# Feed forwards and output projection with the tokens stationary and 1024 weight columns moving

## The chip, the cores and the metric

One core of a Trainium2 chip runs the kernel. The metric is the device time of one execution in microseconds; lower is better. Times before are the median of three runs, beside one execution taken with the hardware profiler.

## What is computed

One layer on 256 tokens of width 2048, all in float32. Feed forwards have a hidden width of 5632.

```python
def swiglu(h, w_gate, w_up, w_down):
    return (jax.nn.silu(h @ w_gate) * (h @ w_up)) @ w_down

x = x + 0.5 * swiglu(rmsnorm(x, ffn1_norm), ffn1_w_gate, ffn1_w_up, ffn1_w_down)
h = rmsnorm(x, mix_norm)
rq, rk, rv, rg, aq, ak, av, iq, ik, iw = split(h @ w_in)
...   # retention on rq, rk, rv gated by rg; attention on the best 64 keys by an index score
x = x + concatenate([ro, ao]) @ w_out
x = x + 0.5 * swiglu(rmsnorm(x, ffn2_norm), ffn2_w_gate, ffn2_w_up, ffn2_w_down)
return rmsnorm(x, final_norm)
```

## The kernel before

Weights stream from DRAM once, in loads of 1 MB (`load`, SyncE's queue, three buffers `raw`). They are used in pieces of up to 1024 columns of 128 rows. Products keep float32 precision by splitting each number in a rounded part and a rest: `split(i)` lets ScalarE write the rounded part `hi` of piece i (L214) and VectorE the rest `lo` (L215), each with five buffers. A product is then hi x hi + hi x lo + lo x hi.

`mm_cols` (L137 with its partner L139, or L136 where a sum ends) does almost all products: a block of 128 weight columns is stationary, and the activations move, transposed, as 512 columns: 256 tokens of the rounded part and 256 of the rest. A 512 column product with the weights' `hi` and a 256 column product with their `lo` make one pair for each k tile and block. The result has the hidden or model columns in the partitions and the tokens along the row; the two halves of its bank are added when it is read. `mm_rows` (L154 to L156) does three small projections of the mix the other way around: 128 tokens are stationary, and 272 or 512 weight columns move.

x lies transposed in eight tiles of two k tiles. A feed forward takes its hidden columns in two halves, each of 11 chunks of 256: gate and up as two accumulators (`evac`: ScalarE copies one half of the bank to `b`, L315, VectorE adds the other, L317), scaling by the norm's row `r_of` (`row_of` builds it with TensorE), Silu, product, and the split of the result (`hs`). After the 11 chunks come eight chunks of 256 model columns (`down`), added to x; in the second half `split_x` and `square_x` make the next norm's inputs, and `add_squares` sums squares over the partitions with TensorE. The mix follows with its projections and small products, then the output projection, the second feed forward and `finish`, which scales x and sends it out in eight transfers.

The order on each engine is the program's: `split` runs four pieces ahead (two at the very start), then `run_step(i)` issues the functions that are due at step i (the work registered with `after`, stages of a function by `yield`), then piece i's products. So a function at step i stands on ScalarE and VectorE behind the split of piece i + 4, and on TensorE between the products of pieces i - 1 and i. PSUM is in two pools, two accumulators of two banks and four single banks, handed out anew for each use.

```python
        while n_split < min(n, i + ahead + 1):
            split(n_split)
            n_split += 1
        run_step(i)
        pieces[i]["mm"](*split_of.pop(i))
```

Of the kernel before, what the change touches and what calls it, by code (L numbers as in the profile page):

```python
# [19 lines left out]
P = 128  # L20
T = 256          # tokens
D = 2048         # model width
KT = D // P      # 16
FF = 5632
NCH = FF // 256  # 22 chunks of 256 hidden columns
HCH = NCH // 2   # 11 chunks in each half
HKT = 2 * HCH    # 22 k tiles in each half
# [18 lines left out]
def layer(ctx: ExitStack, tc: tile.TileContext, a: dict, out: bass.AP):  # L46
# [7 lines left out]
    p_acc = ctx.enter_context(tc.tile_pool(name="p_acc", bufs=2, space=PSUM))  # L54
    p_sm = ctx.enter_context(tc.tile_pool(name="p_sm", bufs=4, space=PSUM))
# [16 lines left out]
    gains = new(one, [P, 4 * KT + NH], F32, "gains")  # L72
    cst = new(one, [P, 4 + NH], F32, "cst")
    x = [new(one, [P, 2, T], F32, f"x{c}") for c in range(KT // 2)]
    xg = {}

# [1 line left out]
    loads = []   # lists of (offset, source)  # L78
# [7 lines left out]
    # a function may be a generator of stages; it yields the steps from one stage to the next  # L86
# [14 lines left out]
    class Chunk:  # L101
        """Where the products of a chunk of columns add up: a bank for each block of 128."""
        acc = None

        def get(self):
            if self.acc is None:
                self.acc = new(p_acc, [P, 2, 512], F32, "acc")
            return self.acc
# [4 lines left out]
    class LastChunk:  # L113
        """The same, with the first block complete before the last piece's products for the second"""

        banks = None

        def bank(self, b):
            if self.banks is None:
                self.banks = two_banks()  # L120
            return self.banks[b]

    def mm_cols(chunk, blocks, kts, rhs, first, last):
        """W[k, 128 cols] stationary; the split activations [k, hi | lo] move."""

        def go(hi, lo):
            order = [(i, b) for i in range(len(kts)) for b in range(blocks)]
            if last and isinstance(chunk, LastChunk):
                order.sort(key=lambda ib: ib[1])
            for i, b in order:  # L130
# [12 lines left out]
    def mm_rows(chunk, n, kts, rhs, first, last):  # L143
        """Tokens stationary; W[k, n cols] moves."""
# [14 lines left out]

    def block(src, l0, l1, width):  # L160
        """k tiles l0 to l1 of a chunk, which lie in DRAM as one block"""
        return src[P * l0 * width:P * l1 * width].rearrange("(p n) -> p n", p=P)

    def stream(src, kts, width, per_load, per_piece, rhs, chunk, maker, arg):
        """One chunk of columns over all its k tiles."""
# [8 lines left out]
        return len(pieces)   # the step after the chunk's last  # L174

    def stream_pair(srcs, rhs, chunks):
        """The first two chunks side by side, while x is loaded."""
        for k0 in range(0, KT, 4):
            w = 2 if k0 == 0 else 4
            parts = []  # L180
            for k in range(k0, k0 + 4, w):
                pre = list(range(k // 2, (k + w) // 2))
                parts += [lambda c=c: load_x(c) for c in pre]
                for m in range(2):
                    off = m * 1024 + (k - k0) * 256
                    at = (k % 8) * 256
                    parts.append((off, block(srcs[m], k // 8 * 8, k // 8 * 8 + 8, 256)[:, at:at + w * 256]))
                    pieces.append(dict(load=len(loads), off=off, n=w * 256, x=pre if m == 0 else [],
                                       mm=mm_cols(chunks[m], 2, list(range(k, k + w)), rhs, k == 0, k + w == KT)))
            loads.append(parts)  # L190
        return len(pieces) - 1, len(pieces)
# [12 lines left out]
    def split(i):  # L204
# [4 lines left out]
        for c in p.get("x", []):  # L209
            split_x(c, 0)  # L210
# [8 lines left out]
    s2 = {}  # L219

    def split_x(c, norm):
        """x * gain of two k tiles, split, for the next projections."""
        t = new(one, [P, 2, 512], F32R, f"xg{c}")
        for j in range(2):
            g = gains[:, norm * KT + 2 * c + j:norm * KT + 2 * c + j + 1]
            S.activation(t[:, j, :T], x[c][:, j], AF.Copy, scale=g)  # L226
            V.scalar_tensor_tensor(t[:, j, T:], x[c][:, j], g, t[:, j, :T].bitcast(F32), op0=OP.mult, op1=OP.subtract)  # L227
        xg[c] = t

    def square_x(c, norm):  # L230
# [671 lines left out]
```

## Time and profile before

| | |
|---|---|
| median of 3 runs | 1932.77 us (1932.54 to 1933.04) |
| the profiled execution's span, first to last instruction | 1931.7 us |
| TensorE busy (matmul records) | 1914.8 us, 99% |
| VectorE, ScalarE busy | 1207.8 us (63%), 924.9 us (48%) |
| read from DRAM | 352.63 MB, 184 GB/s over the span |

The profiled execution's own time is known by its span alone; the median of the runs is 1.07 us longer. Engines are named PE (TensorE matmul), PEld (its weight loads, which overlap the matmuls), DVE (VectorE), ACT (ScalarE), SP (SyncE). A line of a group reads: line of the kernel, engine, operation, written tile <- read tiles, shapes, count, then the busy time in us and the mean of one in ns, then the engine's idle time before them and what ended it. A line of the timeline reads: start in us, length in us, engine, line, operation, count of merged instructions, and in brackets the idle time before it and its releaser. Matmul records overlap, and their ends are modelled.

### The profile page before, as it was taken

The numbers are of one execution on the slowest core, as the hardware profiler recorded it, in microseconds if no ns is written. First come the engines' busy times: TensorE is split into PE (matmuls) and PEld (weight loads), VectorE is DVE, ScalarE is ACT, GpSimd is POOL, SyncE is SP. The second block draws the span as 40 slices with busy tenths as digits, with TensorE's granted clock in tenths as the row PEclk, the third lists the DMA queues.
The fourth block names the chain that finished last, engine by engine and source line by source line (L and its number), as shares of the span: only waits on it lengthen the run. The fifth ranks groups of instructions, "written<-read, shape, count | busy, mean of one in ns | idle before, by whom it ended". The sixth has DMA issues, their size and how long they took to land.

```text
span 1931.7 us, 26692 instructions
## 1 busy us (share of the span) xinstructions
PE 1914.8 (99%) x10936; PEld 1672.2 (87%) x10936; DVE 1207.8 (63%) x1444; ACT 924.9 (48%) x1127; POOL 5.3 (0%) x14
## 2 busy tenths in 40 slices
PE   8999999999999999999999999999999999999997
PEld 7888888888888888988888888888888888888886
DVE  7675655555656666688755766565655556655554
ACT  7444443344444445656544555444443344444442
POOL 0000000000000000000000000000000000000000
PEclk9999999999999999999999999999999999999999
DMA  7555555555555555545544555555555555555552
GB/s 287 187 184 196 178 178 189 197 192 182 194 182 184 180 188 202 177 156 196 175 153 158 187 179 191 182 194 182 189 180 182 194 188 193 187 184 191 179 181 104
DMA packets 53050, 356.44 MB, mean 185 GB/s; under 512 B 6048, under 2 KB 6048, under 8 KB 14144
## 3 DMA queue, kind: packets, MB, share of 16 engines
q1 hardware_dynamic: 52416, 353.52, 53.5%
q8 instruction: 85, 1.39, 0.3%
q0 software_dynamic: 368, 1.19, 0.2%
q14 instruction: 37, 0.30, 0.0%
q10 hardware_dynamic: 144, 0.04, 0.0%
HBM read 352.63 MB, written 2.10 MB: 184 GB/s over the span
## 4 chain that ended last, share of the span: by engine, by line
PE 99%; DVE 0%; DMA 0%; ACT 0%; issue 0%; DVEq 0%
PE acc L137 62%; PE acc L139 30%; PE acc L136 2%; PE acc L155 1%; PE acc L156 1%; PE acc L154 1%; PE sm L137 1%; PE sm L583 0%; PE sm L631 0%; PE sm L139 0%; DVE x L390 0%; DMA gains<-in_gains 0%; PE sm L724 0%; PE sm L700 0%; PE sm L662 0%; PE sm L267 0%
## 5 line engine op out<-in xcount | busy, mean ns | idle before, releaser
L137 PE MATMUL acc<-xg,hi 128*128 128x512 f32 x3504 | 1230.2, 395 | 5.8 <-DVE xg L227 5.8
L215 DVE TENSOR_TENSOR lo<-raw,hi 128x1024 fp32r<-128x1024 f32 (+2 forms) x686 | 817.2, 1194 | 665.9 <-ACT hi L214 664.2
L214 ACT ACTIVATE hi<-raw 128x1024 fp32r<-128x1024 f32 (+2 forms) x686 | 705.8, 1033 | 795.3 <-PE acc L137 754.2
L139 PE MATMUL acc<-xg,lo 128*128 128x256 f32 x3285 | 929.7, 283 | 0.0
L137 PEld LDWEIGHTS acc<-xg,hi 128*128 128x128 f32 x3504 | 652.6, 188 | 149.3 <-ACT hi L214 5.8
L139 PEld LDWEIGHTS acc<-xg,lo 128*128 128x128 f32 x3285 | 618.9, 188 | 5.0 <-DVE lo L215 0.4
L137 PE MATMUL acc<-mid,hi 128*128 128x512 f32 x1620 | 569.0, 398 | 0.0
L139 PE MATMUL acc<-mid,lo 128*128 128x256 f32 x1542 | 433.0, 281 | 0.0
L137 PEld LDWEIGHTS acc<-mid,hi 128*128 128x128 f32 x1620 | 302.0, 188 | 71.0 <-DVE mid L757 0.2
L139 PEld LDWEIGHTS acc<-mid,lo 128*128 128x128 f32 x1542 | 291.3, 189 | 1.6
L325 ACT ACTIVATE s<-e 128x512 f32<-128x512 f32 x44 | 27.8, 632 | 82.1 <-DVE e L323 82.1
L136 PE MATMUL acc<-xg,lo 128*128 128x256 f32 x219 | 61.1, 279 | 0.0
L317 DVE TENSOR_TENSOR e<-acc,b 128x512 f32<-128x512 f32 x88 | 60.1, 683 | 0.0
L315 ACT ACTIVATE b<-acc 128x512 f32<-128x512 f32 x88 | 51.1, 581 | 3.2 <-PE acc L137 3.2
L136 PEld LDWEIGHTS acc<-xg,lo 128*128 128x128 f32 x219 | 41.2, 188 | 5.0
L226 ACT ACTIVATE xg<-x,gains 128x256 fp32r<-128x256 f32 x48 | 21.5, 500 | 41.8 <-DVE x L808 19.5
L490 ACT ACTIVATE b<-e 64x512 f32<-64x512 f32 (+2 forms) x46 | 28.1, 612 | 15.6 <-DVE e L480 15.0
L154 PE MATMUL acc<-hi,xg 128*128 128x512 f32 (+1 forms) x96 | 34.9, 364 | 0.0
L155 PE MATMUL acc<-lo,xg 128*128 128x512 f32 (+1 forms) x96 | 34.5, 359 | 0.0
L156 PE MATMUL acc<-hi,xg 128*128 128x512 f32 (+1 forms) x96 | 34.5, 359 | 0.0
L331 DVE TENSOR_TENSOR e<-e,s 128x512 f32<-128x512 f32 x44 | 30.4, 692 | 1.5
L335 DVE TENSOR_TENSOR mid<-e,mid 128x512 fp32r<-128x512 f32 x44 | 30.1, 685 | 0.0
(149 smaller groups left out, 661.0 us busy)
## 6 DMA issues: line engine op xcount, KB each, us to landing
raw<-in_wgu SPq DMA_DIRECT2D x172, 1024.0 KB, 4.8
raw<-in_wd SPq DMA_DIRECT2D x64, 1024.0 KB, 4.8
raw<-in_wd SPq DMA_DIRECT2D x32, 768.0 KB, 4.2
raw<-in_w_out SPq DMA_DIRECT2D x16, 1024.0 KB, 4.8
raw<-in_w_iq SPq DMA_DIRECT2D x8, 1024.0 KB, 4.8
raw<-in_w_aq SPq DMA_DIRECT2D x8, 1024.0 KB, 4.8
raw<-in_w_rk SPq DMA_DIRECT2D x8, 1024.0 KB, 4.9
raw<-in_w_rq SPq DMA_DIRECT2D x8, 1024.0 KB, 4.9
```

Source lines behind the costliest of these rows:

```text
L136: TE.matmul(acc[:, T:], lhsT=lo[:, c:c + P], rhs=r[:, :T], start=False, stop=False)
L137: TE.matmul(acc, lhsT=hi[:, c:c + P], rhs=r, start=st, stop=sp)
L139: TE.matmul(acc[:, T:], lhsT=lo[:, c:c + P], rhs=r[:, :T], start=False, stop=False)
L154: TE.matmul(o, lhsT=h, rhs=hi[:, i * n:(i + 1) * n], start=st, stop=False)
L155: TE.matmul(o, lhsT=h, rhs=lo[:, i * n:(i + 1) * n], start=False, stop=False)
L156: TE.matmul(o, lhsT=l, rhs=hi[:, i * n:(i + 1) * n], start=False, stop=sp)
L214: S.activation(hi[:, :p["n"]], raw, AF.Copy)
L215: V.tensor_tensor(lo[:, :p["n"]], raw, hi[:, :p["n"]].bitcast(F32), op=OP.subtract)
L315: S.activation(b, acc[:, :, T:], AF.Copy)
L317: V.tensor_tensor(g, acc[:, :, :T], b, op=OP.add)
L331: V.tensor_tensor(u, u, sil[c], op=OP.mult)
L335: V.tensor_tensor(h[:, :, T:], u, h[:, :, :T].bitcast(F32), op=OP.subtract)
```

## The change

The feed forwards and the output projection go over to `mm_wide`: 128 tokens are stationary, 1024 weight columns move as two products of 512 into the two banks of a token tile. A piece is one k tile of 1024 columns. A chunk is 512 gate and 512 up columns; a feed forward has two parts of 6 and 5 chunks, and `down` and the output projection have two halves of 1024 model columns. PSUM is two fixed sets of four banks, used in turn; in the mix one set serves as the two accumulators (`pair`) and the other as the four single banks (`small`).

Results now lie by token. `hidden` multiplies them with the norm's factor per token, so no row is needed there, and TensorE transposes the gated product back, a step later, into the chunk's own set, for the split. x lies by token too: x is loaded a second time in that layout, `grow` adds to it, squares are summed by ScalarE along the row, and `turn_x` transposes it into the banks just read, for `split_x`. For norm 0 the transposed x is loaded into passing buffers. The output has another layout, and the last gain is loaded broadcast over the partitions.

```diff
-    p_acc = ctx.enter_context(tc.tile_pool(name="p_acc", bufs=2, space=PSUM))
-    p_sm = ctx.enter_context(tc.tile_pool(name="p_sm", bufs=4, space=PSUM))
+    psum = ctx.enter_context(tc.tile_pool(name="psum", bufs=1, space=PSUM))
...
+    sets = [[new(psum, [P, 2, 512], F32, f"set{s}{t}") for t in range(2)] for s in range(2)]
...
+    def mm_wide(acc, _, kts, rhs, first, last):
+        def go(hi, lo):
+            for i, kt in enumerate(kts):
+                r = rhs(kt)
+                st, sp = first and i == 0, last and i == len(kts) - 1
+                for t in range(2):
+                    h, l = r[:, t * P:(t + 1) * P], r[:, T + t * P:T + (t + 1) * P]
+                    for n, (w, m) in enumerate(((h, hi), (h, lo), (l, hi))):
+                        for c in range(2):
+                            TE.matmul(acc[t][:, c], lhsT=w, rhs=m[:, (2 * i + c) * 512:(2 * i + c + 1) * 512],
+                                      start=st and n == 0, stop=sp and n == 2)
...
+    def turn_x(c, norm, bank):
+        v = bank.rearrange("p (j t) -> p j t", j=2)
+        for j in range(2):
+            for t in range(2):
+                TE.transpose(v[:, j, t * P:(t + 1) * P], x[t][:, (2 * c + j) * P:(2 * c + j + 1) * P], ident)
+        split_x(c, norm, v)
...
+    def grow(acc, c, scale, norm):
+        for t in range(2):
+            for i in range(2):
+                xs = x[t][:, halves(2 * c + i)]
+                V.scalar_tensor_tensor(xs, acc[t][:, i], scale, xs, op0=OP.mult, op1=OP.add)
+            if norm is not None:
+                square_x(norm, t, c * 1024, 1024)
+
+    def to_next(norm, c, acc, step):
+        for i in range(4):
+            after(step + i // 2, lambda i=i: turn_x(4 * c + i, norm, acc[i // 2][:, i % 2]))
...
+                def hidden(acc=acc, cc=cc):
+                    ht = []
+                    for t in range(2):
+                        r = r_tok[norm][:, t:t + 1]
+                        s = new(tmp, [P, W], F32, "s")
+                        S.activation(s, acc[t][:, 0], AF.Silu, scale=r)
+                        ht.append(new(tmp, [P, W], F32, "e", 3))
+                        V.scalar_tensor_tensor(ht[t], acc[t][:, 1], r, s, op0=OP.mult, op1=OP.mult)
                     yield 1
+                    for q in range(2):
+                        v = acc[q][:, 0].rearrange("p (j t) -> p j t", j=2)
+                        for j in range(2):
+                            for t in range(2):
+                                TE.transpose(v[:, j, t * P:(t + 1) * P], ht[t][:, halves(2 * q + j, P)], ident)
+                        h = big(F32R, (P, 2, 512))
+                        S.activation(h[:, :, :T], v, AF.Copy)
+                        V.tensor_tensor(h[:, :, T:], v, h[:, :, :T].bitcast(F32), op=OP.subtract)
+                        hs[2 * cc + q] = h
+                after(end, hidden)
...
+            for d in range(2):
+                acc = sets[next_set()]
+                end = stream(wd[part][d], list(range(4 * n)), 1024, 2, 1, rhs_h, acc, mm_wide, None)
...
+                after(end, down)
+                if part == 1 and not last:
+                    to_next(next_norm, d, acc, end + 1)
...
+    def finish(acc):
+        for t in range(2):
+            for i in range(2):
+                xs = x[t][:, halves(2 + i)]
+                V.scalar_tensor_tensor(xs, acc[t][:, i], 0.5, xs, op0=OP.mult, op1=OP.add)
+                square_x(3, t, halves(2 + i).start, 512)
+        rstd_tok(3)
+        for t in range(2):
+            r = r_tok[3][:, t:t + 1]
+            xs = [x[t][:, halves(c, 1024)] for c in range(2)]
+            S.activation(xs[0], xs[0], AF.Copy, scale=r)
+            V.scalar_tensor_tensor(xs[1], xs[1], r, last_gain[1], op0=OP.mult, op1=OP.mult)
+            for c in range(2):
+                nc.sync.dma_start(out[t][:, halves(c, 1024)], xs[c])
...
     def first_squares():
-        for c in range(KT // 2):
-            square_x(c, 0)
-            yield 1
+        for t in range(2):
+            nc.sync.dma_start(x[t], a["x"][t])
+        yield 4
+        for t in range(2):
+            for c in range(2):
+                square_x(0, t, 1024 * c, 1024)
+                yield 1
+        rstd_tok(0)
```

## Rows read from the trace of the kernel before

**Rows 1.** The page: span, part 1 (busy us, share, instructions), part 4.

```profile
span 1931.7 us, 26692 instructions
...
PE 1914.8 (99%) x10936; PEld 1672.2 (87%) x10936; DVE 1207.8 (63%) x1444; ACT 924.9 (48%) x1127; POOL 5.3 (0%) x14
...
PE 99%; DVE 0%; DMA 0%; ACT 0%; issue 0%; DVEq 0%
```

**Rows 2.** Windows: stretch, length, busy us per engine, clock, DMA, GB/s.

```profile
1400.00:1900.00 500.00, 500.00 (x2846) 436.54 (x2845) 287.00 (x301) 224.34 (x255) 0.00 (x0) 1.00 0.54 185
```

**Rows 3.** Timeline, TensorE: `mm_cols` at a chunk's end, then `mm_rows`.

```profile
302.94 0.62 PE L137 MATMUL acc<-mid,hi 128*128 128x512 f32 x2
...
985.15 0.39 PE L156 MATMUL acc<-hi,xg 128*128 128x512 f32 x1
...
986.07 0.40 PE L154 MATMUL acc<-hi,xg 128*128 128x512 f32 x1
986.30 0.40 PE L155 MATMUL acc<-lo,xg 128*128 128x512 f32 x1
...
986.54 0.40 PE L156 MATMUL acc<-hi,xg 128*128 128x512 f32 x1
...
992.81 0.40 PE L156 MATMUL acc<-hi,xg 128*128 128x512 f32 x1
```

**Rows 4.** Timeline, TensorE: four transposes (`ret_mix`) between products of `mm_cols`.

```profile
1068.90 0.28 PE L139 MATMUL acc<-xg,lo 128*128 128x256 f32 x1
1069.03 0.60 PE L750 MATMUL sm<-ident,mid 128*128 128x128 f32 x4
...
1069.70 0.28 PE L139 MATMUL acc<-xg,lo 128*128 128x256 f32 x1
```

**Rows 5.** Timeline, ScalarE and VectorE: after a piece of `mm_rows`; at a chunk's end.

```profile
993.24 1.06 ACT L214 ACTIVATE hi<-raw 128x1024 fp32r<-128x1024 f32 x1 [1.72 <-PE acc L156]
...
1299.80 1.06 ACT L214 ACTIVATE hi<-raw 128x1024 fp32r<-128x1024 f32 x1 [1.84 <-PE acc L137]
...
1300.89 1.23 DVE L215 TENSOR_TENSOR lo<-raw,hi 128x1024 fp32r<-128x1024 f32 x1 [1.67 <-ACT hi L214]
1302.03 0.68 DVE L317 TENSOR_TENSOR e<-acc,b 128x512 f32<-128x512 f32 x1
```

**Rows 6.** Timeline: TensorE released by VectorE; eight operations of VectorE in a row.

```profile
1093.81 0.69 DVE L757 TENSOR_TENSOR mid<-e,mid 128x512 fp32r<-128x512 f32 x1 [0.70 <-ACT mid L756]
...
1094.56 0.19 PEld L137 LDWEIGHTS acc<-mid,hi 128*128 128x128 f32 x1 [0.22 <-DVE mid L757]
...
1922.94 4.87 DVE L390 TENSOR_TENSOR x<-x,sm 128x512 f32<-128x512 f32 x8 [0.67 <-PE sm L267]
```

**Rows 7.** Groups of ScalarE and VectorE by line; one table load of the timeline.

```profile
L546 ACT ACTIVATE mid<-acc,r_tok 128x512 f32<-128x512 f32 x4 | 2.5, 675 | 0.0
...
L431 DVE SCALAR_TENSOR_TENSOR mid<-mid,mid 128x1024 f32<-128x1024 f32 x3 | 3.6, 1217 | 0.0
...
1053.42 1.28 ACT L566 ACT_TABLE_LOAD   x1
```

**Rows 8.** Timeline of the start: ScalarE's first split of x, TensorE's first matmul.

```profile
4.33 0.91 ACT L226 ACTIVATE xg<-x,gains 128x256 fp32r<-128x256 f32 x2 [1.66 <-DMA gains<-in_gains]
...
5.81 0.80 PE L137 MATMUL acc<-xg,hi 128*128 128x512 f32 x1 [5.81 <-DVE xg L227]
```

**Rows 9.** Timeline of the end; last line: GB/s in 40 slices of 1915 to 1932.

```profile
1918.01 0.39 PE L137 MATMUL sm<-mid,hi 128*128 128x512 f32 x1
...
1920.34 0.38 DVE L278 TENSOR_SCALAR sum_v<-sm 128x1 f32<-128x1 f32 x2 [0.92 <-PE sm L273]
...
1923.65 4.51 SPq L391 DMA_DIRECT2D out_T<-x  x8
...
GB/s 0 0 0 0 0 0 0 0 0 0 0 0 0 0 0 0 0 0 0 0 0 0 246 386 366 386 395 362 376 390 366 400 371 386 386 121 0 0 0 0
```

**Rows 10.** Windows, a stretch near the start, columns as in group 2.

```profile
12.00:30.00 18.00, 18.00 (x105) 15.77 (x104) 17.04 (x28) 15.15 (x24) 0.00 (x0) 1.00 0.91 341
```

More of the change, by code (lines that the diff above doesn't have):

```diff
@@ L69, in big, with next_set, pair, small @@
         return new(mid, list(shape), dt, "mid")
-    gains = new(one, [P, 4 * KT + NH], F32, "gains")
+    gains = new(one, [P, 3 * KT + NH], F32, "gains")
     cst = new(one, [P, 4 + NH], F32, "cst")
-    x = [new(one, [P, 2, T], F32, f"x{c}") for c in range(KT // 2)]
+    x = [new(one, [P, D], F32, f"x{t}") for t in range(2)]
     xg = {}
+    sets = [[new(psum, [P, 2, 512], F32, f"set{s}{t}") for t in range(2)] for s in range(2)]
+    turn = [0, 0, 0]
+    mix_sets = []
+    def next_set():
+        turn[0] ^= 1
+        return turn[0] ^ 1
+    def pair():
+        turn[1] += 1
+        return mix_sets[0][turn[1] % 2]
+    def small():
+        turn[2] += 1
+        return mix_sets[1][turn[2] // 2 % 2][:, turn[2] % 2]
     loads = []
@@ L111, in bank @@
             return self.get()[:, b]
[L113 to L121, printed above, removed]
     def mm_cols(chunk, blocks, kts, rhs, first, last):
         def go(hi, lo):
[L127 to L130, printed above, removed]
+            for i, b in [(i, b) for i in range(len(kts)) for b in range(blocks)]:
                 acc = chunk.bank(b)
@@ L268, in row_of, with rstd_tok @@
         return ps[:, :T]
-    def add_squares(ps, sq, first, last):
-        for t in range(2):
-            TE.matmul(ps[t][:, 0:1], lhsT=sq[:, t * P:(t + 1) * P], rhs=ones[:, 0:1], start=first, stop=last)
-    def rstd_tok(norm, ps):
+    def rstd_tok(norm):
         v = new(tmp, [P, 2], F32, "sum_v", 1)
-        for t in range(2):
-            V.tensor_scalar(v[:, t:t + 1], ps[t][:, 0:1], 1.0 / D, EPS, op0=OP.mult, op1=OP.add)
+        s, k = squares[norm]
+        V.tensor_reduce(v, s[:, :, :k[0]], axis=AX.X, op=OP.add)
+        V.tensor_scalar(v, v, 1.0 / D, EPS, op0=OP.mult, op1=OP.add)
         r_tok[norm] = new(one, [P, 2], F32, f"r_tok{norm}")
         rsqrt(r_tok[norm], v, 2)
-    def two_banks():
-        return [new(p_sm, [P, 512], F32, "sm") for _ in range(2)]
     def rstd(norm):
-        ps = two_banks()
-        add_squares(ps, s2[norm], True, True)
-        rstd_tok(norm, ps)
+        rstd_tok(norm)
         row = yield from row_of(r_tok[norm])
@@ L366, in ffn @@
                 after(end, down)
-        return end
-    def scale_x(c):
-        for j in range(2):
-            kt = 3 * KT + 2 * c + j
-            S.activation(x[c][:, j], x[c][:, j], AF.Copy, scale=gains[:, kt:kt + 1])
-    def finish(chunk):
-        c = KT // 2 - 1
-        sq = half_k("sq")
-        ps = two_banks()
-        add_squares(ps, s2[3], True, False)
-        for j in range(2):
-            for half in range(2):
-                V.scalar_tensor_tensor(x[c][:, j], chunk.bank(j)[:, half * T:(half + 1) * T], 0.5, x[c][:, j],
-                                       op0=OP.mult, op1=OP.add)
-            S.activation(sq[:, j], x[c][:, j], AF.Square)
-            add_squares(ps, sq[:, j], False, j == 1)
-        rstd_tok(3, ps)
-        scale_x(c)
-        row = yield from row_of(r_tok[3])
-        for c in range(KT // 2):
-            V.tensor_tensor(x[c], x[c], two(row), op=OP.mult)
-            nc.sync.dma_start(out[:, 2 * c:2 * c + 2], x[c])
+                if part == 1 and not last:
+                    to_next(next_norm, d, acc, end + 1)
@@ L578, in index_scores @@
         w = P if t == 0 else T
-        ps = [new(p_sm, [P, 512], F32, "sm") for _ in range(2)]
+        ps = [small() for _ in range(2)]
         for i in range(n):
@@ L657, in attend @@
         yield 2
-        ps = new(p_sm, [P, 512], F32, "sm")
+        ps = small()
         for j in range(2):
@@ L682, in k_tok @@
             ret["ktok"] = big(shape=(P, NH, P))
-        ps = new(p_sm, [P, 512], F32, "sm")
+        ps = small()
         for i in range(4):
@@ L719, in ret_o @@
             ret["o", n] = big(shape=(P, NH, P))
-        ps = new(p_sm, [P, 512], F32, "sm")
+        ps = small()
         for i in range(4):
@@ L746, in ret_mix @@
     def ret_mix(c):
-        ps = new(p_sm, [P, 512], F32, "sm")
+        ps = small()
         for j in range(2):
@@ L900 @@
     got = r.results[0]["out_T"]
[L901 removed]
+    return np.ascontiguousarray(got.reshape(1, T, D))
```

202 lines of the change are left out of this document (87 added, 115 removed).

## The prediction

> **What bounds the kernel now.** The page first: TensorE is busy in 99% of the span and the chain that ended last is 99% TensorE [rows 1]. So every nanosecond put into or taken out of TensorE's stream counts in full, and work on the other engines counts only where TensorE waits for it. Next the pace of that stream. In 500 us in the middle of the second feed forward there are 2846 matmuls, 1423 pairs of a 512 column and a 256 column product [rows 2]: 0.3514 us for a pair, though the records in the groups are 0.28 and 0.40 us long (they overlap, so a record's length is no cost). Then the one place where the kernel already does what the change does elsewhere, tokens stationary and 512 weight columns moving (`mm_rows`): from 985.15 to 992.81 us 33 steps from start to start, 0.2321 us each [rows 3]. Last the views of ScalarE and VectorE at a chunk's end [rows 5], because the change makes TensorE wait for them there.
>
> The sum is made against the profiled span of 1931.7 us; the median of the runs is 1932.77, so 1.07 us lie around the span, and I add them unchanged.
>
> **Matmuls.** A unit is one k tile times 1024 weight columns, or its like: 6144 moved columns both before (8 pairs of 768) and after (12 of 512). Each feed forward has 11 x 16 units for gate and up and 2 x 44 for down, the output projection 2 x 16: 560 in all. Before 8 x 0.3514 = 2.811 us [rows 2], after 12 x 0.2321 = 2.785 us [rows 3]: 0.026 us x 560 = **14.6 us less**. The differences from `mm_rows` are the same stationary for up to four products running (two there) and two banks in turn; two neighbours of `mm_cols` in different banks started 0.62 - 0.40 = 0.22 us apart, and steps of 0.24 occur in `mm_rows` [rows 3]. With 0.2308 and 0.2345 as bounds of the mean it is 23 us less to 1 more.
>
> The Trainium skill has a rule for the same thing, "TensorE: Matmul & The Clock Gate", section Back-to-back issue gap: N / 2.4 + 2.5 ns, 215.8 ns for 512 and 109.2 for 256. By it the unit would go from 2.600 to 2.590 us and the sum be 9 us higher; the trace does not agree with it for these products (232.1 ns), and the rows decide.
>
> **Transposes added on TensorE.** Eight for each of 22 chunks (`hidden`), and four in each of 16 calls of `turn_x` (8 after the first feed forward, 8 after the output projection): 176 + 64 = 240. Four of them stand between two matmuls in [rows 4]: from one 256 column product to the next there are 0.80 us, against 0.351 for a pair without them, so 0.112 us each. 240 x 0.112 = **26.9 us more**, all in the stream. Bound from below 0.109 (their own pitch: 0.60 less a record of 0.27, over 3), 26.2 us.
>
> Removed: for norms 0 and 2 the four records of `row_of`, for norms 0 to 2 four of `add_squares`, 20 x 0.11 (the pitch in [rows 4]), and a wait of 0.22 us for the last `mix` [rows 6], which is now needed 8 pieces later: **2.4 us less**.
>
> **The wait for the gated products.** This is new. `split(e+4)` is issued before the functions of step e, so on ScalarE the copy `hi` stands ahead of the two Silu, and on VectorE the subtraction `lo` ahead of the two products `ht`. And `hi` can't start before the chunk's last piece has been read (five buffers). From [rows 5], with time 0 where TensorE starts the next piece: `hi` starts 0.20 (993.24, where the next matmul starts at 992.81 + 0.23), `lo` 1.09 later at 1.29, the next VectorE operation 1.14 later at 2.43; the products for t=0 and t=1 start 0.60 apart (eight in 4.87, the last 0.68 long, [rows 6]), so the second starts at 3.03, ends at 3.72, and TensorE takes it up 0.06 later [rows 6], at 3.78. The Silu (about 0.68 each, like the scaled copy out of PSUM in [rows 7]) fit beside `lo`. TensorE has one piece of 2.785 as cover, then the first transpose, 0.11, and needs t=1 at 2.90. It stands 0.88 us, 22 times: **19.4 us more**. Bounds: 0.6 (products back to back with `lo`, no latency) to 1.6 (one more operation of 0.69 in between), 13 to 35 us.
>
> Two chunks have a table load of 1.28 [rows 7] ahead of their first Silu (after the square roots of norms 0 and 2), which puts the second product at 4.47: 0.75 more each. One (the second) has an operation of the position tables, 1.22 [rows 7], ahead of it on VectorE. **2.6 us more** (0 to 4).
>
> **The wait for x.** `turn_x` needs the third of the four sums in `grow` (t=1, first half): start 2.43 + 2 x 0.60, end 4.32, seen at 4.38; cover 2.90; 1.48 us, four times: **5.9 us more** (4 to 10). At the mix the transposed halves are needed a piece later, and there `split_x` alternates ScalarE and VectorE on one PSUM bank (about half a us for each operation, two in 0.91 [rows 8]) behind two Squares of 1024. Followed through the queues, TensorE loses 0.3 us if both engines may read a bank at once and 2.7 if they take turns. No row decides it; I take **2.0**, nearer to the upper end, since any delay in those queues adds to it.
>
> The Trainium skill speaks against this step: "PSUM — Partial Sum Buffer", section PSUM bank collisions raise a hardware error, has it that two engines must not be in one bank at a time, two readers included. No run here shows it; by it the term is 2.7.
>
> **The first piece of the output projection.** Its set holds, in the half for t=1, the last rg chunk. That is read by `hi`, `b`, `lo`, `e` in order and free at about 0.1 + 2.23 + 0.68 = 3.0 [rows 5]; t=0 covers 6 x 0.232 = 1.39. **1.7 us more.** Before, another buffer was free.
>
> **Start and end.** The first `hi` is 1024 wide instead of 512 and behind the same `xg` [rows 8]: the stream starts about **0.7 us** later. x comes a second time, 2.1 MB from step 4 in SP's queue, ahead of the load for pieces 12 and 13: 6 us at 341 GB/s [rows 10]. Loads are issued as buffers come free, some ten pieces (28 us) ahead of TensorE; that lead hides it. Were it gone, 6 us. The last gain is loaded by ScalarE's queue into free buffers, 16 steps ahead: nothing. At the end the first output leaves 5.4 us after the last matmul (1918.24 to 1923.65, [rows 9]); after, two sums (to 1.5), Square with its sum (to about 2.5), then the small steps and a product of 1.06 before the first output, where today 3.3 lie from the first small step (1920.34) to the first output, `diag` and `row_of` among them: about the same 5.4. Then 2.1 MB at 386 GB/s in both. **0**, within 2.
>
> ScalarE and VectorE lose work (per 256 hidden columns four operations of VectorE and two of ScalarE), but with TensorE busy in 99% of the span [rows 1] it hardly waits for them today: nothing gained.
>
> **Sum.** -14.6 + 26.9 - 2.4 + 19.4 + 2.6 + 5.9 + 2.0 + 1.7 + 0.7 = +42.2 us: 1931.7 + 1.07 + 42.2 = **1975 us**. With independent bounds this case holds 1958 to 1995.
>
> **Rivals.**
> - *The stream gets faster.* If the stationary, the same for four and then two products, or the change of banks took away what a 512 column product needs beyond its columns (512 at the granted level of 2.4 GHz is 0.2133 us, and the windows grant 1.00 throughout), 6720 products would save 0.0188 each, 126 us: 1849. It turns the sign as soon as a product takes less than 0.2321 - 42.2/6720 = 0.2258. For it: the stationary changes only twice in six products. Against it: `mm_rows` has two equal ones running, and the step between them (986.07 to 986.30) is no shorter [rows 3]. Chance 0.09 for a faster kernel, 0.03 for one that lands within 0.2%. By the gap that the Trainium skill gives ("TensorE: Matmul & The Clock Gate", Back-to-back issue gap) for this stream alone it would be about 1865 us.
> - *The waits at the chunk ends don't come.* If TensorE found the products ready (the transposes' inputs done within a piece), 19.4 + 2.6 + 5.9 go: 1947. For it: ScalarE and VectorE idle for over half of each piece. Against it: the order in their queues, seen at today's chunk ends [rows 5]. 0.12.
> - *A transpose costs its record.* 0.272 instead of 0.112 us in the stream: 38 us on top, 2013. Against it [rows 4]; for it, only that eight run in a row after a wait. 0.05. The Trainium skill, "TensorE: Matmul & The Clock Gate", Part 4: PE-mode transpose, gives about 275 ns for one inside a kernel; the record's length agrees (0.27), the pitch doesn't.
>
> The forecast has 0.71. The range of 1945 to 2000 holds it and the second rival, 0.83 to 0.86 in all. What a measurement can tell from no change is about 0.2%, 3.9 us: faster 0.09, within it 0.03, slower 0.88.
>
> **What would show it.** Matmul records fall from 10936 to 8900 (8960 + 36 gone, 6720 + 240 new). In a window of gate and up, starts 0.232 apart: right; under 0.226: the first rival. TensorE's idle time before the transposes of `hidden`, released by VectorE's products: 22 times 0.9 us, and 1.5 before those of `turn_x`. TensorE's clock stays at 1.00. VectorE's busy time falls without any gain. I am wrong if the pace is another, or if ScalarE or VectorE take the chunk's end ahead of the split.

## The result, and the profile after

The changed kernel takes 2034.5 us (median of 4 runs, 2027.3 to 2035.3) against 1932.9 for the kernel before beside it: a ratio of 1.0517, 95% interval 1.0501 to 1.0533. It is slower, as forecast, but by 102 us and not by 42, and lies outside the range of 1945 to 2000. The profiled execution has a span of 2032.1 us against 1931.7 [rows 1], 100.4 us more; the working below is made on the spans.

The page first: span, part 1 (busy time, share, instructions), the granted clock in 40 slices of part 2, and the chain of part 4.

```profile
span 2032.1 us, 21925 instructions
...
PE 1945.7 (96%) x8900; PEld 1595.7 (79%) x8900; DVE 1049.2 (52%) x1140; ACT 881.4 (43%) x1008; POOL 5.3 (0%) x14
...
PEclk9999999999999988999999999999999999999999
...
PE 91%; DVE 4%; ACT 3%; issue 2%; DMA 0%; DVEq 0%; SPq 0%; ACTq 0%
```

TensorE is no longer busy throughout: 86 us of the span are empty, where before it was 17 [rows 1]. The chain that was TensorE's for 99% now runs through VectorE and ScalarE for 7%. The 8900 matmul records are those forecast. The clock's row shows two slices at 8 in the middle (a 9 stands for anything from 0.90 on); the forecast had a clock of 1.00 throughout.

Where the time went, by stage. The stages are cut where the first product of each part starts in the two timelines; the last row counts from one step behind the start of the last product:

| stage | before, us | after, us | more |
|---|---|---|---|
| start, to the first matmul | 5.8 | 8.1 | 2.3 |
| first feed forward | 746.2 | 773.8 | 27.6 |
| mix | 332.3 | 362.6 | 30.3 |
| output projection | 90.8 | 105.6 | 14.8 |
| second feed forward | 743.1 | 769.2 | 26.1 |
| after the last matmul | 13.5 | 12.7 | -0.8 |

The mix, whose products the change leaves alone, is the stage that lost most (two of the eight stops shown below lie in it, those of the second half of `down`). That was the first sign that something was missing in the sum. The view of waits says on whom TensorE's weight loads stood (engine, tile, line, what they waited for: us in all, times, longest):

```profile
PEld set L249 <- DVE xg L241: 35.0, 8, 5.1
PEld set L353 <- DVE e L347: 28.5, 43, 1.8
...
PEld set L249 <- DVE x L319: 6.8, 8, 1.3
...
PEld set L675 <- DVE mid L690: 4.8, 2, 2.6
...
PEld set L675 <- ACT mid L678: 3.4, 2, 1.9
...
PEld set L174 <- DVE e L584: 2.4, 1, 2.4
```

L353 are the transposes of the gated products (forecast), L249 those of x behind the sums of L319 (forecast), L174 the first piece of the output projection (forecast). The largest row, L249 behind `split_x` (L241), and the rows of L675 in the mix were in no part of the prediction. This is how the largest looks in the timeline of all engines, at the end of the first half of the first feed forward:

```profile
712.57 2.48 DVE L319 SCALAR_TENSOR_TENSOR x<-set,x 128x512 f32<-128x512 f32 x4
...
713.88 1.06 ACT L260 ACTIVATE mid<-x 128x1024 f32<-128x1024 f32 x1 [0.98 <-DVE x L319]
713.90 0.33 PE L249 MATMUL set<-ident,x 128*128 128x128 f32 x1 [0.89 <-DVE x L319]
...
714.50 0.55 PE L249 MATMUL set<-ident,x 128*128 128x128 f32 x3 [0.27 <-DVE x L319]
...
715.08 1.06 ACT L260 ACTIVATE mid<-x 128x1024 f32<-128x1024 f32 x1
...
716.13 1.04 ACT L230 ACTIVATE hi<-raw 128x1024 fp32r<-128x1024 f32 x1
717.08 0.45 ACT L240 ACTIVATE xg<-set,gains 128x256 fp32r<-128x256 f32 x1
...
719.37 0.48 DVE L241 SCALAR_TENSOR_TENSOR xg<-set,gains,xg 128x256 fp32r<-128x256 f32 x1 [0.54 <-ACT xg L240]
719.91 1.11 PE L249 MATMUL set<-ident,x 128*128 128x128 f32 x4 [4.86 <-DVE xg L241]
```

Two blocks of x are transposed in this step, the first into bank 0 of a set's tile, the second into bank 1 of the same tile. The second four start only at 719.91, released by the last `split_x` operation on bank 0 (719.37 to 719.85), although nothing had read their own bank since the sums of L319. And `split_x` itself stands on ScalarE behind two Squares and the next weight split (to 717.08). Start to start that is 5.13 us (714.78 to 719.91), and one step later another 3.71. It happens at four places, the two ends of `down` ahead of the mix and the two of the output projection.

At each of them the granted clock falls. Windows (stretch, length, then busy us of PE, PEld, DVE, ACT, POOL with counts, granted clock, DMA share, GB/s):

```profile
712.00:720.00 8.00, 1.98 (x10) 1.05 (x9) 5.15 (x8) 4.97 (x9) 0.00 (x0) 0.90 0.34 122
720.00:728.50 8.50, 6.25 (x20) 4.90 (x20) 2.48 (x4) 2.37 (x4) 0.00 (x0) 0.69 0.28 112
728.50:740.00 11.50, 10.32 (x36) 8.43 (x37) 3.04 (x6) 3.54 (x5) 0.00 (x0) 0.70 0.07 14
740.00:770.00 30.00, 30.00 (x134) 24.86 (x133) 13.61 (x12) 11.67 (x11) 0.00 (x0) 1.00 0.56 205
```

TensorE was busy for 2 of the 8 us up to 720; then the mean clock of the next two stretches is 0.69 and 0.70, which is a part of each at 1.2 and the rest at 2.4 GHz.

The other stop that was not forecast is in the mix: `small()` now hands out the two banks of one tile in turn, and `attend`'s transposes into one bank (L675) wait for readers of the other (L690):

```profile
1034.93 0.68 DVE L690 TENSOR_TENSOR mid<-set,mid 128x512 fp32r<-128x512 f32 x1
1035.66 0.14 PEld L675 LDWEIGHTS set<-ident,mid 128*128 128x128 f32 x1 [2.63 <-DVE mid L690]
```

And the pace of the stream, in the timeline of TensorE, has two values: with x stationary four products start within 1.10 - 0.40 us, 0.233 apart, with the gated products stationary within 1.07 - 0.39, 0.227 apart. Over the whole trace the steps between two L174 products, those under 0.25 us, have means of 0.2325 for `xg` and 0.2268 for `mid`.

```profile
215.13 1.10 PE L174 MATMUL set<-hi,xg 128*128 128x512 f32 x4
...
314.83 1.07 PE L174 MATMUL set<-hi,mid 128*128 128x512 f32 x4
```

### The profile page after: what moved, and what is told of

Its sections match the earlier page's. It is cut to its first block, busy times and chain, and to the rows that moved or that the text cites. A ratio compares the mean times of both kernels' runs of the same rounds, so it can differ in the third digit from the quotient of the medians.

```text
span 2032.1 us, 21925 instructions
## 1 busy us (share of the span) xinstructions
PE 1945.7 (96%) x8900; PEld 1595.7 (79%) x8900; DVE 1049.2 (52%) x1140; ACT 881.4 (43%) x1008; POOL 5.3 (0%) x14
## 4 chain that ended last, share of the span: by engine, by line
PE 91%; DVE 4%; ACT 3%; issue 2%; DMA 0%; DVEq 0%; SPq 0%; ACTq 0%
PE set L174 73%; PE set L140 8%; PE set L142 4%; DVE e L347 1%; ACT s L345 1%; PE set L353 1%; ACT hi L230 1%; PE set L158 1%; PE set L159 1%; PE set L157 1%; DVE lo L231 1%; DVE x L319 0%; PE set L249 0%; DVE xg L241 0%; PE set L605 0%
## 5 line engine op out<-in xcount | busy, mean ns | idle before, releaser
L231 DVE TENSOR_TENSOR lo<-raw,hi 128x1024 fp32r<-128x1024 f32 (+1 forms) x668 | 815.7, 1222 | 914.3 <-ACT hi L230 913.4
L230 ACT ACTIVATE hi<-raw 128x1024 fp32r<-128x1024 f32 (+1 forms) x668 | 705.8, 1057 | 1029.0 <-PE set L174 852.3
L174 PE MATMUL set<-hi,xg 128*128 128x512 f32 x2816 | 778.8, 397 | 8.1 <-ACT hi L230 8.1
L174 PEld LDWEIGHTS set<-hi,xg 128*128 128x128 f32 x2816 | 531.3, 189 | 131.7 <-ACT hi L230 8.1
L174 PE MATMUL set<-hi,mid 128*128 128x512 f32 x1664 | 453.7, 393 | 2.0 <-DVE e L584 2.0
L174 PE MATMUL set<-lo,xg 128*128 128x512 f32 x1408 | 443.6, 396 | 0.1
L174 PEld LDWEIGHTS set<-hi,mid 128*128 128x128 f32 x1664 | 315.4, 190 | 68.0 <-DVE e L584 2.4
L174 PEld LDWEIGHTS set<-lo,xg 128*128 128x128 f32 x1408 | 266.3, 189 | 63.8 <-DVE lo L231 1.2
L174 PE MATMUL set<-lo,mid 128*128 128x512 f32 x832 | 259.3, 393 | 0.0
L140 PE MATMUL set<-xg,hi 128*128 128x512 f32 x688 | 251.6, 406 | 0.0
L174 PEld LDWEIGHTS set<-lo,mid 128*128 128x128 f32 x832 | 158.2, 190 | 33.5
L249 PE MATMUL set<-ident,x 128*128 128x128 f32 x64 | 14.4, 351 | 37.5 <-DVE xg L241 33.1
L353 PE MATMUL set<-ident,e 128*128 128x128 f32 x176 | 28.9, 286 | 16.6 <-DVE e L347 16.6
L353 PEld LDWEIGHTS set<-ident,e 128*128 128x128 f32 x176 | 19.5, 141 | 30.2 <-DVE e L347 28.5
L249 PEld LDWEIGHTS set<-ident,x 128*128 128x128 f32 x64 | 9.2, 173 | 42.2 <-DVE xg L241 35.0
```

The lines of the kernel that those rows point to most:

```text
L140: TE.matmul(acc, lhsT=hi[:, c:c + P], rhs=r, start=st, stop=sp)
L174: TE.matmul(acc[t][:, c], lhsT=w, rhs=m[:, (2 * i + c) * 512:(2 * i + c + 1) * 512], start=st and n == 0, stop=sp and n == 2)
L230: S.activation(hi[:, :p["n"]], raw, AF.Copy)
L231: V.tensor_tensor(lo[:, :p["n"]], raw, hi[:, :p["n"]].bitcast(F32), op=OP.subtract)
L249: TE.transpose(v[:, j, t * P:(t + 1) * P], x[t][:, (2 * c + j) * P:(2 * c + j + 1) * P], ident)
L353: TE.transpose(v[:, j, t * P:(t + 1) * P], ht[t][:, halves(2 * q + j, P)], ident)
```

## The experiments

**Theory.** Beside the waits of the prediction, three things act: a wait goes by the whole two-bank PSUM tile, so what is written into one bank stands behind readers of the other (at the four ends of a model half, and in the mix); the stops bring the lower clock with them; and the place of the stationary tile in SBUF sets the pace. **Rivals:** the queues of ScalarE and VectorE or the banks themselves make the stops; the clock falls for another reason; the pace follows from the operands' roles.

**1. The order of the transposes.** In `to_next`, both blocks of a step are transposed, then both are split:

```diff
-        split_x(c, norm, v)
+        return v
...
-        for i in range(4):
-            after(step + i // 2, lambda i=i: turn_x(4 * c + i, norm, acc[i // 2][:, i % 2]))
+        def both(t):
+            vs = [turn_x(4 * c + 2 * t + i, norm, acc[t][:, i]) for i in range(2)]
+            for i in range(2):
+                split_x(4 * c + 2 * t + i, norm, vs[i])
...
+            after(step + t, lambda t=t: both(t))
```

> The four transposes of a step's second block of x now stand ahead of the two splits instead of between them; nothing else changes. Theory (a wait goes by the whole two-bank PSUM tile, so the second four stand behind the first block's split): at the four ends of a model half the waits of 5.1 us, and those of 3.6 to 3.7 us a step later, fall under 1 us; 4 x (5.1 + 3.7 - 1) = 31 us less. If the half clock after them comes from those stops, its eight stretches of 6.8 us there go too, and the kernel is at 1975 to 1990 us. Rival (the stops cost their length alone and the half clock has another cause): the stretches stay, 1998 to 2010. Rival (the second four wait for their own bank's readers, the sums of x): waits and time stay as they are, 2025 to 2035.

Measured: 1984.6 us, 49.9 less than the changed kernel (ratio to before 1.0267, 1.0237 to 1.0296). The same place in the timeline of all engines, and the windows of the same stretches (columns as above):

```profile
716.50 0.98 PE L249 MATMUL set<-ident,x 128*128 128x128 f32 x7 [0.26 <-DVE x L319]
...
717.24 0.71 PE L174 MATMUL set<-hi,mid 128*128 128x512 f32 x2
...
720.08 1.03 PE L249 MATMUL set<-ident,x 128*128 128x128 f32 x8
```

```profile
712.00:720.00 8.00, 6.85 (x34) 5.33 (x33) 4.41 (x6) 6.16 (x9) 0.00 (x0) 1.00 0.38 133
720.00:728.50 8.50, 8.50 (x44) 7.12 (x42) 4.87 (x9) 4.10 (x9) 0.00 (x0) 1.00 0.36 123
728.50:740.00 11.50, 11.50 (x52) 9.52 (x51) 7.66 (x7) 6.09 (x7) 0.00 (x0) 1.00 0.62 231
```

The four transposes into the other bank follow the first four without a stop, eight in a row start 0.109 us apart ((1.03 - 0.27) / 7), and the clock stays at 1.00. The stops ahead of L249, start to start, sum to 42.5 us in the changed kernel and to 7.3 here; the eight steps that lost their stop still take 0.109 each, 0.9 in all, so the stops were 34.4 us. The time fell by 49.9. The difference of 15.5 us is what the stretches at half clock took beyond the stops. The changed kernel has seven such stretches of 6.8 us at the four places (the expectation counts eight), and here they are gone with the stops. Counted in the changed kernel's own trace, the steps in these seven, without the stops, are about 17 us longer than at full clock. So the rival by which the clock falls for another reason doesn't hold at these places, and the rival of their own bank's readers is out, since the second four no longer wait though those readers are the same.

**2. Single banks.** One set is four tiles of one bank each:

```diff
-    sets = [[new(psum, [P, 2, 512], F32, f"set{s}{t}") for t in range(2)] for s in range(2)]
+    class Banks:
+        def __init__(self, name):
+            self.banks = [new(psum, [P, 512], F32, f"{name}{c}") for c in range(2)]
+        def __getitem__(self, at):
+            return self.banks[at[1]][:, :]
+    sets = [[Banks(f"set0{t}") for t in range(2)],
+            [new(psum, [P, 2, 512], F32, f"set1{t}") for t in range(2)]]
```

> One of the two PSUM sets is cut into four tiles of one bank each; it serves the second half of the model's columns at the end of the first feed forward and of the output projection, and all small products of the mix. The order of the work is that of the changed kernel. Theory (waits go by PSUM tile): the 5.1 and 3.7 us waits go at the two places that this set serves and stay at the other two; the mix's own transposes and products, which stand 1.5 to 2.7 us behind readers of a neighbour bank (11 us in all), wait under 0.5 us; 2 x 8 + 11 us and the half clock behind them, 1985 to 2005 us. Rival (the hardware or the engines' queues make these waits, not the tile): no change, 2025 to 2035.

Measured: 1995.2 us (1.0321, 1.0291 to 1.0351), 39 less. From its view of waits:

```profile
PEld set L258 <- DVE xg L250: 17.5, 4, 5.1
```

Four waits where the changed kernel had eight, 17.5 us for 35.0: they are gone at the two places that this set serves and unchanged at the other two. No transpose of `attend` waits for a reader any more. So it is the tile, as the program's waits see it, and neither the bank nor the queues: order of the work and engines are those of the changed kernel. The mix has 337.2 us, against 349.0 in experiment 1, where the ends of `down` were already free: 11.8 us for the mix's own small products. The granted clock is 1.00 through the mix in both runs. In the changed kernel two of these waits also bring stretches of 3.4 us at half clock, about 2.7 us more.

**3. The gated products a piece later.**

```diff
-                    yield 1
+                    yield 2
```

> The transposes of the gated products stand two pieces behind their chunk instead of one; nothing else changes. Theory of the prediction (TensorE waits at 22 chunk ends for SiLU and product): the 22 waits of about 1.0 us go, 2005 to 2015 us. Rival (what is late next is the split of the transposes or of the weights, or the stream makes up the wait): under 8 us less, 2020 to 2035.

Measured: 2006.0 us (1.0377, 1.0347 to 1.0407), 28.5 less; by the spans (2005.6) 26.5. Start to start, the steps into and within the transposes of `hidden` sum to 48.1 us in the changed kernel (18.1 + 30.0) and to 21.9 here (5.1 + 16.8): 26.2 us of waiting, all of it gone, and nothing took its place. The wait in the changed kernel, in the timeline of all engines:

```profile
199.32 1.40 DVE L347 SCALAR_TENSOR_TENSOR e<-set,r_tok,s 128x512 f32<-128x512 f32 x2
...
200.12 0.33 PE L353 MATMUL set<-ident,e 128*128 128x128 f32 x1 [0.30 <-DVE e L347]
...
200.78 0.98 PE L353 MATMUL set<-ident,e 128*128 128x128 f32 x7 [0.33 <-DVE e L347]
```

TensorE waits for the first product and again for the second, about 1.0 us together at 19 of the 22 chunk ends; the prediction counted only the later one, which holds both.

**4. The place in SBUF.** In the changed kernel `xg` and the pieces `hi` and `lo` start 128 bytes apart within 512, the gated products (`mid`) and the pieces at the same place (worked out from the sizes of the tiles; the trace has no addresses). An unused tile at the end of the pool `one` moves pieces and `mid` together:

```diff
+    def pad():
+        G.memset(new(one, [P, 224], F32, "pad"), 0.0)
+    after(40, pad)
```

> An unused tile of 896 bytes a partition behind the small tiles moves the weights' pieces and the gated products in SBUF, so that the stationary x and the moving weights start at the same place within 1024 bytes, as the gated products and the weights do; nothing else changes. Theory (the 0.2325 us of a product with x stationary against 0.2267 with the gated products stationary comes from where the tiles lie in SBUF): products with x stationary start 0.227 apart, 4224 x 0.0057 = 24 us less, about 2005 to 2012 us. Rival (it comes from the order of the operands or from what runs beside them): 0.2325 stays, 2025 to 2035.

Measured: 2001.0 us (1.0351, 1.0306 to 1.0396), 33.5 less; the two runs are 1997.4 and 2004.6, the trace is of the first. Four products with x stationary (timeline of TensorE):

```profile
215.71 1.07 PE L174 MATMUL set<-hi,xg 128*128 128x512 f32 x4
```

The mean is now 0.227 us for `xg` too. The pace accounts for 4224 x 0.0057 = 24 us. The rest goes with fewer stretches of half clock: five in the middle of the run, where the changed kernel has ten. Three of the four places have one here and two there; why, no run shows.

Three more kernels asked what "the same place" means. With a tile of 384 bytes (96 columns, as in the diff) it is the same within 512 but not within 1024; with 128 bytes (32 columns) the two lie 256 apart; with 320 bytes (80 columns) 64 apart.

```diff
-        G.memset(new(one, [P, 224], F32, "pad"), 0.0)
+        G.memset(new(one, [P, 96], F32, "pad"), 0.0)
```

> An unused tile of 384 instead of 896 bytes: the stationary x and the moving weights then start at the same place within 512 bytes and not within 1024. Theory (places count within 512 bytes): the pace with x stationary is 0.227 us and the time that of the 896-byte tile, 1995 to 2005 us. Rival (they count within 1024 bytes): 0.2325 us and 2025 to 2035 us.

> An unused tile of 128 bytes: the stationary x and the moving weights start 256 bytes apart within 512, where the changed kernel has them 128 apart and the tile of 384 bytes 0 apart. Theory (only the same place within 512 bytes gives the faster pace): products with x stationary start 0.230 us apart or more, 2020 to 2035 us. Rival (the same place within 256 bytes is enough): 0.227 us and about 2005 us.

> An unused tile of 320 bytes: the stationary x and the moving weights start 64 bytes apart within 512. Theory (the exact place counts): products with x stationary start 0.230 us apart or more, 2020 to 2035 us. Rival (a near place is enough): 0.227 us and about 2005 us.

Measured: 2007.3, 2006.2 and 2037.4 us (the last two single runs), with means of 0.227, 0.227 and 0.233 us. TensorE's timeline with 128 bytes, then with 320:

```profile
216.08 1.07 PE L174 MATMUL set<-hi,xg 128*128 128x512 f32 x4
```

```profile
215.27 1.10 PE L174 MATMUL set<-hi,xg 128*128 128x512 f32 x4
```

My expectation for 128 bytes was wrong: 256 bytes apart is as good as 0. Of the distances seen, 0 and 256 give the faster pace, 64 and 128 the slower.

**5. The same move in the kernel before.** Small tiles of 384 bytes in all (`top8`, `stat1`, `rstat`) are made at their first use, and so lie behind `xg` instead of ahead of it; for `top8`:

```diff
-    top8 = [new(one, [P, 8], F32, f"top8_{t}") for t in range(2)]
...
-            V.max(top8[t], score[t])
+            V.max(late(f"top8_{t}", [P, 8]), score[t])
...
```

> The kernel before, with three small tiles of 384 bytes in all laid behind x instead of ahead of it, so that x and the weights' pieces start at the same place within 512 bytes; the order of the work is untouched. Theory (place counts for the one that is stationary against the one that moves, whichever they are): a pair of products with x moving goes from 0.351 to 0.340 us or less, 1860 to 1915 us. Rival (with the weights stationary place is worth nothing, as the pair of 0.3523 us with gated products moving, which already lie so, suggests): 1930 to 1938 us.

Measured: 1938.2 us, slower by 0.28% (ratio 1.0028, 1.0015 to 1.0041). In the window of [rows 2]:

```profile
1400.00:1900.00 500.00, 500.00 (x2833) 434.06 (x2832) 286.53 (x300) 223.38 (x255) 0.00 (x0) 1.00 0.54 185
```

A pair of products goes from 0.3514 to 0.3530 us. In the same kernel `mm_rows`, with x stationary, goes from 0.2321 [rows 3] to 0.227 (its timeline has a product every 0.227 us). So the place is worth something where the tokens are stationary and 512 weight columns move, and nothing where the weights are stationary: the gain belongs to the new form of the work, and the same move gives the kernel before nothing.

**6. Together.** The four edits of 1 to 4 in one kernel, and then also the transposes of x one piece later at three of the four places:

```diff
-                to_next(next_norm, d, acc, end + 1)
+                to_next(next_norm, d, acc, end + 2 - d)
-        to_next(2, d, acc, end + 1)
+        to_next(2, d, acc, end + 2)
```

> The four edits tried one at a time, together: both transposes of a step ahead of their splits, one set as four single banks, the gated products a piece later, the unused tile. Theory (the four causes are separate: 50 us from the order of the transposes, 28 from the later step, 28 to 30 from the place in SBUF, 12 more in the mix from the single banks): 1910 to 1922 us, faster than the kernel before (1932.9). Rival (what one edit frees another wait takes: the same PSUM tiles, or the split of the weights is late next): 1925 to 1945 us.

> As the four edits together, and the transposes of x stand one piece later at three of the four ends of a model half (not at the start of the mix, whose fourth piece needs them). Theory (the 1.2 to 1.3 us and 0.6 us that the first transposes still wait for the sums of x are the sums' own length): 3 x 1.8 = 5 us less than the four edits alone, 1905 to 1917 us. Rival (the wait only moves to the next thing that reads the sums, or the second half's transposes then meet the second set): within 2 us of the four alone.

Measured: 1919.2 us (ratio to before 0.9932, 0.9917 to 0.9947) and 1913.2 us (0.9898, 0.9882 to 0.9915). Both beat the kernel before. The page of the second:

```profile
PE 1887.8 (99%) x8900; PEld 1577.7 (83%) x8900; DVE 1047.9 (55%) x1140; ACT 876.3 (46%) x1008; POOL 5.6 (0%) x15
...
PE 98%; DVE 1%; ACT 0%; DMA 0%; issue 0%; DVEq 0%; SPq 0%; ACTq 0%
```

TensorE is the bound again. The four gains found one at a time sum to 151 us, what they bring together is 115, since experiments 1, 2 and 4 overlap at the ends of `down` and in the clock.

**7. One stop put back.** The kernel with the four edits, with the transposes between their splits again at one place:

```diff
+            if norm == 1 and c == 0:
+                for i in range(2):
+                    split_x(2 * t + i, norm, turn_x(2 * t + i, norm, acc[t][:, i]))
+                return
```

> The four edits together (1919.2 us), with the transposes of x between their splits again at one place alone, the end of the first half of the first feed forward. Theory (the stops of 5.1 and 3.7 us bring TensorE's lower clock with them): both stops and about 13 us at half clock behind them come back there, the time grows by more than the stops' 8.8 us, to 1930 to 1933 us. Rival (the stops cost their length and the half clock is another matter): 1927 to 1928.5 us, with no stretch of half clock there. Rival (with the gated products a piece later and the second set in single banks the stops no longer come): 1919 us.

Measured: 1931.1 us (10 runs, 1927.7 to 1932.8) against 1919.2 (1918.9 to 1922.0). Windows of that place, and TensorE's timeline in the third stretch:

```profile
687.00:692.50 5.50, 0.87 (x4) 0.45 (x4) 3.34 (x6) 3.61 (x6) 0.00 (x0) 0.80 0.21 83
692.50:700.00 7.50, 5.38 (x20) 4.33 (x20) 1.75 (x5) 2.54 (x5) 0.00 (x0) 0.69 0.40 140
704.00:711.00 7.00, 7.00 (x26) 5.56 (x25) 2.08 (x3) 2.00 (x3) 0.00 (x0) 0.76 0.00 0
```

```profile
704.19 1.91 PE L183 MATMUL set<-hi,mid 128*128 128x512 f32 x4
```

The stops of 5.13 and 3.71 us are back, and the products behind them start 0.427 us apart for a while and not 0.227. One place costs 11.9 us by the medians, of which 8.6 are the stops (8.84 less the 0.22 that the same steps take without a wait). The remaining 3.3 us is the clock: in the profiled execution the steps between products that are longer than 0.227 us behind the two stops (up to 0.57, most of them 0.427) add up to 3.0 us. The theory's 1930 to 1933 holds the median, though it had 13 us at half clock; the length of the slow stretches differs between executions (here 6.8 and 3.4 us), and so does the time.

## Why the prediction was wrong

The sign and the mechanisms named were right; the size was not, because two places were left out and one constant was taken to stay. Term by term, forecast and measured, on the spans:

| term | forecast, us | measured, us | from |
|---|---|---|---|
| products | -14.6 | -26.2 | 4224 x 0.2325 + 2496 x 0.2267, less 560 x 2.811 |
| transposes | +26.9 | +26.2 | 240 x 0.109 |
| removed | -2.4 | not separable | |
| wait for gated products, tables | +22.0 | +26.2 | experiment 3 |
| first wait for x | +5.9 | +6.0 | 7.3 left in experiment 1, less 8 steps without a wait (1.3) |
| `split_x` at the mix | +2.0 | 0; 1.3 where the stops are gone | experiment 1: a step of 1.38 there |
| first piece of the output projection | +1.7 | +2.1 | a step of 2.38, less 0.23 |
| start | +0.7 | +2.3 | stages; the first product came at 6.9 to 10.1 us in the runs of the new form |
| end | 0 | -0.8 | stages |
| second transposes of a step | not seen | +34.4 | experiment 1 |
| half clock with them | not seen | +15.5 to 17 | experiment 1; the seven stretches in the trace |
| small products of the mix | not seen | +11.8 | experiments 1 and 2 |
| half clock with these and at the output projection's first piece | not seen | +4.3 | three stretches of 3.4 us in the trace |

The place of experiment 7 lost 3.3 us to the clock, with one stretch of 6.8 and one of 3.4 us. Three of the changed kernel's four places have two of 6.8 us, the fourth has one. With -2.4 for what was removed the measured terms give +99 to +101 of 100.4, so no large term is missing.

**The step that failed is "The wait for x".** It followed ScalarE and VectorE through their queues for the first four transposes of a step, and got that wait right to 0.1 us. It then let the second four of the same step go free, because they write another bank, and spoke of delays only for the mix's need of the halves a piece later. But the set is one tile of two banks, and experiment 2 shows that the wait goes by the tile. The prediction even had the queue that makes this dear (two Squares ahead of `split_x`). What it lacked was the question, for each write into PSUM: which tile is it part of, and who still reads any of it? The kernel before had a clue: its `LastChunk` has its banks as separate tiles.

**"The clock stays at 1.00" failed with it.** In the kernel before, from 12 us to the last product of `down`, no two products started more than 0.42 us apart, and the granted clock was 1.00 there. The forecast carried that over to a kernel for which it had itself 27 stops of 0.9 to 1.7 us. At the ends of `down`, those of 1.3 us left it at 1.00 (experiment 1), those of 5.1 and 3.7 us did not. In the changed kernel it also fell behind two waits of 2.3 and 2.7 us in the mix and behind one of 2.4 us at the first piece of the output projection. These are the windows of the first and the last (columns as above):

```profile
1011.00:1016.00 5.00, 5.00 (x25) 4.37 (x23) 0.00 (x0) 1.04 (x3) 0.00 (x0) 0.66 0.03 7
...
1147.00:1153.00 6.00, 4.94 (x15) 3.90 (x16) 2.89 (x4) 1.58 (x2) 0.00 (x0) 0.72 0.15 61
```

Another wait of 2.4 us in the mix left it at 1.00, and a chunk end with a wait of 1.8 us did so in the changed kernel and not in experiment 1 (3.4 us at half clock from 109.6). So the length of a stop alone does not decide it.

**The mix was taken as untouched.** The change replaced its four separate small tiles by halves of two, and the sum had no line for that.

**Right:** that the products would gain little and the transposes eat it; the pitch of a transpose, 0.109, the lower of the two values read from [rows 4], so the rival with the record's length is out (the Trainium skill, "TensorE: Matmul & The Clock Gate", Part 4: PE-mode transpose, has about 275 ns; records here are 271 ns, starts 109 apart). The wait at the chunk ends came as derived from the two queues, 1.06 us for the 0.88 (the 26.2 less 2.9, over 22), with longer ones at the first two chunk ends and at the second feed forward's first (0.9, 1.1 and 0.9 more, 2.9 for the forecast 2.6); the rival without them (1947) is out.

**Half right:** the pace. 0.2321 was forecast for all products; those with x stationary have it (0.2325), those with the gated products stationary are at 0.2267. The first rival, a faster stream that turns the sign below 0.2258, was thus not far from what the work can do: with all products at 0.227 and the waits gone, the changed form is at 1913 us. No mean is below 0.2267 (single steps go down to 0.223); by the formula in the Trainium skill (same page, section Back-to-back issue gap), given there for an isolated matmul, 512 columns are estimated at 215.8 ns, and the trace does not agree. One argument for that rival was that the stationary block changes only twice in six products; the page of the profile has a weight load for every matmul, 8900 of each (PEld and PE).

**The term left open, two readers of one bank.** The prediction took 2.0 us for `split_x` at the mix, between 0.3 if both engines may read a PSUM bank at once and 2.7 if they take turns. They take turns: ScalarE's second operation waits 1.3 us for VectorE's first, with single banks too. At the start `split_x` reads x from SBUF into the same kind of tile `xg`, and there ScalarE's two operations run in a row while VectorE's first begins:

```profile
3.99 0.91 ACT L240 ACTIVATE xg<-e,gains 128x256 fp32r<-128x256 f32 x2 [1.31 <-DMA gains<-in_gains]
4.53 0.88 DVE L241 SCALAR_TENSOR_TENSOR xg<-e,gains,xg 128x256 fp32r<-128x256 f32 x2 [3.52 <-ACT xg L240]
...
718.86 0.47 ACT L240 ACTIVATE xg<-set,gains 128x256 fp32r<-128x256 f32 x1 [1.33 <-DVE xg L241]
```

So the turns go with the source in PSUM and not with the tile that is written. That agrees with the Trainium skill, "PSUM — Partial Sum Buffer", section PSUM bank collisions raise a hardware error, by which two engines must not be in one bank at a time, two readers included. In the changed kernel the stops hide the term; where they are gone TensorE loses 1.3 us in one step there.

## What to carry to other kernels

Before two banks are made one PSUM tile, list for each bank who reads it last and what is next written into the other: in this program the whole tile is what a wait sees, so the write stands behind both. Work that TensorE takes from ScalarE and VectorE at a chunk's end belongs one piece later than the data seem to allow, where the cover is a whole piece and not what the queues leave of it. A change that looks lost by a sum of waits may be worth its repair: here five small edits took 121 us off, and the form of the work that was 5.2% slower became 1.0% faster than what it replaced.

## What the runs showed of the hardware that I had not expected

- With tokens stationary and 512 fp32r columns moving, the pace depends on where the two tiles start in SBUF: 0.227 us when their places differ by 0 or 256 bytes within 512, 0.2325 and 0.233 when they differ by 128 or 64. With the weights stationary the like move gained nothing (0.3514 to 0.3530 us for a pair).
- With stops of TensorE of 5.1 and 3.7 us come stretches of 3.4 and 6.8 us at the lower level of the granted clock (1.2 GHz), in which a 512 column product takes 0.427 us instead of 0.227. Some waits of 1.8 to 2.7 us bring a stretch of 3.4 us too, others don't.
